# Hybrid decoder layer: the meta tokens' probabilities of four heads turned by one transpose, and the reciprocal sums turned in pairs of heads

## The chip, the cores and the metric

The kernel runs on one core of one Trainium2 chip. The metric is the device time of one execution in microseconds (us); a version's time is the median of several runs.

## The reference

One decoder layer in float32 over 1024 tokens, with 16 learned meta tokens put ahead of them. One input projection feeds two mixers side by side: a chunkwise retention (4 heads) and a sparse attention (8 query heads of 64, one shared key and value head). For every query the sparse attention picks 256 keys by an indexer's score and softmaxes over these alone. An output projection and a squared-ReLU MLP follow. What the change touches is the last line of the attention:

```
logits = jnp.where(valid[:, :, None, :], logits + bias, NEG)
p = jax.nn.softmax(logits, axis=-1)
return jnp.einsum('bchk,bckd->bchd', p, v_sel)
```

The kernel does not gather: it masks the keys that were not selected and works over all earlier keys. So for a block of 128 queries the probabilities P are a 128 x n matrix per head, and the output is P times the values, divided by the row sums of P. The first 16 columns of P belong to the meta tokens, which every query sees.

## The kernel before, in words

**Precision.** Matmuls take a reduced float32 format (fp32r), so most operands are split into a high and a low half, and products are summed from two or three matmuls. The values are kept as `vv`, where a row is (high half | low half), 128 columns. A product with `vv` as the stationary operand gives a 128-row result whose upper and lower 64 rows are added at the end.

**Units of the attention.** The 1024 queries are 8 blocks (i = 0 to 7) and the 8 heads are 2 groups of four (g), which makes 16 units. Each unit has two parts. `attend_p(i, g)` makes P of four heads: matmuls (L580, L581), a masked sum with a running minimum on DVE (L582), an exponential with row sums on ACT (L589), and at the end the reciprocals of the four row sums (L592). `attend_v(i, g)` applies the values. Per tile of keys it transposes the four heads' P on PE (L607), rounds the result to the high half on ACT (L615), takes the rest as the low half on DVE (L616), and multiplies both with `vv` (L617, L619) into one PSUM accumulator `pv`.

**The meta tile.** The first tile of every unit, k = 0, holds the 16 meta tokens (b = 8). Its four transposes have 16 columns each and give a 16 x 512 tile. The high half lies in rows 0 to 15 of a 128 x 512 buffer `pm` and the low half in rows 32 to 47; the rest of `pm` is zero from a memset. `vv[:, 8]` has the meta values in the same two row groups, so that one matmul does both halves. This matmul opens the accumulator (`start=True`); those of all the other tiles come behind it.

**The tail of a unit.** Four transposes (L623) spread the four reciprocals, 128 equal columns each, over a 128 x 512 PSUM tile `rb`. Then for each of two halves: ACT copies one half of `pv` into `ytmp` (L629), DVE adds the other (L630), and DVE multiplies with the reciprocals into the output `y` (L631). `ytmp` is a tile in the pool `small` under a tag with a single buffer.

**Order of the work.** Unit u's `attend_p` is issued together with unit u-1's `attend_v` and, in 10 of the rounds, with one piece of the output projection (`out_piece`, L669 to L671: 24 matmuls of 512 columns). A helper `spread` interleaves their steps. The rounds u = 2, 3, 6 and 8 have no such piece. On top of that the framework orders the instructions of each engine itself, by priority and readiness in its own simulation, and hands out the buffers of a tag; the resulting order on each engine is fixed. PSUM has 8 banks: 3 for `psA` (scores), 5 for `psB` (`pv`, transposes, `rb`, the projection). The two units of block 0 run their `attend_v` side by side in round 2.

**Set-up.** `small_proj` makes `vv` early, for b = 8 from the meta tokens' projection (L283 to L286). `rsqrt(kss, 9)` (L425) norms the keys. The bias load (L433) is one DMA on SP's queue.

Of the kernel before, what the change touches and what calls it, by code (L numbers as in the profile page):

```python
# [9 lines left out]
F32 = mybir.dt.float32  # L10
F32R = mybir.dt.float32r
BF = mybir.dt.bfloat16
I32 = mybir.dt.int32
AF = mybir.ActivationFunctionType
ALU = mybir.AluOpType
# [5 lines left out]
NM = 16  # L21
ML = 32
# [59 lines left out]
def layer(ctx, tc, x, meta, norm1_w, w_in, ret_w, q_w, k_w, rel, w_out, norm2_w, w1, w2,  # L82
          ident_d, pack_d, hot_d, out, gam):
    nc = tc.nc
    const = ctx.enter_context(tc.tile_pool(name="const", bufs=1))
    wp = ctx.enter_context(tc.tile_pool(name="wp", bufs=1))
    small = ctx.enter_context(tc.tile_pool(name="small", bufs=2))
# [6 lines left out]
    big = stage.enter_context(tc.tile_pool(name="p1", bufs=1))  # L94
# [11 lines left out]
    def page(shape, dt, name):  # L106
        return pg.tile(shape, dt, tag="pg", name=name, bufs=8)
# [7 lines left out]
    def row(name, shape=(128, D)):  # L115
        return big.tile(list(shape), F32, tag="row", name=name, bufs=3)
# [10 lines left out]
    ident = const.tile([128, 128], F32, name="ident")  # L127
# [10 lines left out]

    def rsqrt(ms, k, f=1.0, P=128):
        y = small.tile([128, k], F32, name="rs_y", tag=f"rsy{k}", bufs=1 if k == 9 else 4)  # L140
        nc.gpsimd.tensor_tensor(y[:P], ms, epst[f][:P, :k] if isinstance(f, float) else f, op=ALU.add)
        nc.gpsimd.tensor_tensor(y[:P], y[:P], nhalf[:P, :k], op=ALU.pow)
        return y

    def norm_T(src, P, dst, u=None):
        ss = small.tile([128, 1], F32, name="ss")
        if u is None:
            u = row("u")
        nc.scalar.activation(u[:P, :D], src, AF.Square, scale=D ** -0.5, accum_out=ss[:P])
        r = rsqrt(ss[:P], 1, 1.0, P)  # L150
        nc.vector.scalar_tensor_tensor(u[:P, :D], src, r[:P], nrow[:P], op0=ALU.mult, op1=ALU.mult)
# [109 lines left out]
    NS = 200  # L261
    kn = big.tile([128, 9, 64], F32, name="kn")
    vv = kp_.tile([128, 9, 128], F32R, name="vv")
    nc.vector.memset(vv[:, 8].bitcast(F32), 0.0)
    absw = px.tile([128, NB, 8], F32, name="absw")
    sgnw = px.tile([128, NB, 8], F32, name="sgnw")
    w8 = px.tile([128, NB, 8], F32, name="w8")
    kss = const.tile([128, 9], F32, name="kss")
    nc.vector.memset(kss, 1.0)

    def small_proj(b, hs, ls):
        P = NM if b == 8 else 128
        if b == 8:
            s = proj_meta(hs, ls, 0, NS, "oh", 3)
        else:
            ps = psA()
            proj(ps, b, hs, ls, 0, NS)
            s = big.tile([128, NS], F32, name="smp", tag="fg", bufs=2)
            nc.scalar.activation(s, ps[:, :NS], AF.Copy)
        jk64 = jk[:, :64]  # L280
        nc.scalar.activation(jk64[:P], s[:P, 72:136], AF.Square, scale=0.125, accum_out=kss[:P, b:b + 1])
        nc.vector.tensor_copy(kn[:P, b], s[:P, 72:136])
        nc.scalar.activation(vv[:P, b, 0:64], s[:P, 136:200], AF.Copy)  # L283
        nc.vector.tensor_tensor(vv[:P, b, 64:128], s[:P, 136:200], vv[:P, b, 0:64].bitcast(F32), op=ALU.subtract)
        if b == 8:
            nc.scalar.activation(vv[ML:ML + NM, b], vv[:NM, b].bitcast(F32), AF.Copy)  # L286
        if b < 8:
            nc.vector.tensor_scalar(w8[:, b], s[:, 64:72], 8.0 ** -0.5, None, op0=ALU.mult)
            nc.vector.scalar_tensor_tensor(absw[:, b], w8[:, b], -1.0, w8[:, b], op0=ALU.mult, op1=ALU.max)
            nc.scalar.activation(sgnw[:, b], w8[:, b], AF.Sign)  # L290
        return s
# [127 lines left out]
    ap_ = att.enter_context(tc.tile_pool(name="att", bufs=1, side="right"))  # L419
    knh = ap_.tile([128, KW], F32R, name="knh")  # L420
    knl = ap_.tile([128, KW], F32R, name="knl")
    bias = ap_.tile([128, 8, WIN], F32, name="bias")
    pm = ap_.tile([128, 512], F32R, name="pm")
    nc.gpsimd.memset(pm.bitcast(F32), 0.0)
    kr = rsqrt(kss, 9)  # L425
    for b in range(9):
        P = NM if b == 8 else 128
        nc.vector.scalar_tensor_tensor(kn[:P, b], kn[:P, b], kr[:P, b:b + 1], kgain[:P], op0=ALU.mult, op1=ALU.mult)
# [2 lines left out]
        key_T([(kn[:, b], 128) for b in range(4 * t, 4 * t + 4)], NM + 512 * t, knh, knl, -1.0)  # L431
    gap = gd[:]
    nc.sync.dma_start(bias, bass.AP(tensor=gap.tensor, offset=gap.offset + 127, ap=[[8 * L - 1, 128], [L, 8], [1, WIN]]))  # L433


    yrd = dr.tile([128, NB, 512], F32, name="yrd")
# [79 lines left out]
    for b in range(NB):  # L516
# [9 lines left out]
        r = rsqrt(ssq, 8, 64.0)  # L526
# [9 lines left out]
    for i in range(NB):  # L536
        n = ncol[i]
# [3 lines left out]
    at = {}  # L541
    kc = [0]
# [19 lines left out]
    def attend_p(i, g):  # L562
        n = ncol[i]
        win = wins[i]
        mb = at["m"][:, g]
        u = 2 * i + g
        nc.gpsimd.tensor_tensor(mb[:, :, :win], bias[:, 4 * g:4 * g + 4, WIN - win:],
                                sc[i][:, None, n - win:].to_broadcast([128, 4, win]), op=ALU.add)
        P = []
        sums = small.tile([128, 4], F32, name="sums")  # L570
        rs = small.tile([128, 4], F32, name="rs")
        for hh in range(4):
            per = 4 if i < 3 else 2
            if hh % per == 0:
                pp2 = (page if u < 4 or u % 4 >= 2 and i >= 3 else page_b)([128, per, n if i < 7 else 1056], F32, "P")
            p = pp2[:, hh % per]
            mn = small.tile([128, len(segs[i])], F32, name="mn", tag=f"mn{len(segs[i])}")
            for k, (c0, w, last) in enumerate(segs[i]):
                ps = psA()
                nc.tensor.matmul(ps[:, :w], qst[i][:, 4 * g + hh, :], knh[:, c0:c0 + w], start=True, stop=False)  # L580
                nc.tensor.matmul(ps[:, :w], qst[i][:, 4 * g + hh, :], knl[:, c0:c0 + w], start=False, stop=True)  # L581
                nc.vector.tensor_tensor_reduce(  # L582
                    out=p[:, c0:c0 + w], in0=ps[:, :w], in1=mb[:, hh, :win] if last else sc[i][:, c0:c0 + w],
                    scale=1.0, scalar=3e38, op0=ALU.add, op1=ALU.min, accum_out=mn[:, k:k + 1])
            m1 = mn
            if len(segs[i]) > 1:
                m1 = small.tile([128, 1], F32, name="m1")
                nc.vector.tensor_reduce(m1, mn, axis=mybir.AxisListType.X, op=ALU.min)
            nc.scalar.activation(p[:, :n], p[:, :n], AF.Exp, scale=-1.0, bias=m1, accum_out=sums[:, hh:hh + 1])  # L589
            P.append(p)  # L590
            yield
        nc.vector.reciprocal(rs, sums)  # L592
        res[i, g] = P, rs

    res = {}

    def attend_v(i, g):
        P, rs = res.pop((i, g))
        if g == 0:
            ydsa[i] = p2["p"].tile([128, 4, 128], F32, tag="yd", name="yd", bufs=4) if i else ap_.tile([128, 4, 128], F32, name="yd0")  # L600
        y = ydsa[i]
        pv = psB()
        tiles = [(8, 0, NM)] + [(b, NM + 128 * b, 128) for b in range(i + 1)]
        for k, (b, k0, kp) in enumerate(tiles):
            tp = psB()
            for hh in range(4):
                nc.tensor.transpose(tp[:kp, 128 * hh:128 * hh + 128], P[hh][:, k0:k0 + kp], ident)  # L607
            if "h" not in at:
                at["h"] = [page([128, 4, 512], F32R, "ph")]
            kc[0] += 1  # L610
            e = kc[0] % 2
            ph, pl = at["h"][e // 2][:, e % 2], at["h"][e // 2][:, 2 + e % 2]
            if b == 8:
                ph, pl = pm, pm[ML:]
            nc.scalar.activation(ph[:kp], tp[:kp], AF.Copy)  # L615
            nc.vector.tensor_tensor(pl[:kp], tp[:kp], ph[:kp].bitcast(F32), op=ALU.subtract)  # L616
            nc.tensor.matmul(pv, vv[:, b, :], ph, start=k == 0, stop=False)  # L617
            if b < 8:
                nc.tensor.matmul(pv, vv[:, b, :], pl, start=False, stop=k == len(tiles) - 1)  # L619
            yield  # L620
        rb = psB()
        for hh in range(4):
            nc.tensor.transpose(rb[:, 128 * hh:128 * hh + 128], rs[:, hh:hh + 1].to_broadcast([128, 128]), ident)  # L623
        r4 = rb.rearrange("p (c e n) -> p c e n", c=2, e=2)
        p4 = pv.rearrange("p (c e n) -> p c e n", c=2, e=2)
        tmp = small.tile([128, 2, 128], F32, name="ytmp", tag="ytmp", bufs=1)
        for e in range(2):
            a, z = (slice(0, 64), slice(64, 128)) if e == 0 else (slice(64, 128), slice(0, 64))
            nc.scalar.activation(tmp[a], p4[z, :, e], AF.Copy)  # L629
            nc.vector.tensor_tensor(tmp[a], p4[a, :, e], tmp[a], op=ALU.add)  # L630
            nc.vector.tensor_tensor(y[a, 2 * g:2 * g + 2], r4[a, :, e], tmp[a], op=ALU.mult)  # L631

    nrow = const.tile([128, D], F32, name="nrow2", tag="nrow")
    nc.sync.dma_start(nrow, bcast(norm2_w, D))
# [194 lines left out]
    for u in range(2, 2 * NB):  # L829
        i, g = u // 2, u % 2  # L830
# [73 lines left out]
    big = ctx.enter_context(tc.tile_pool(name="p3", bufs=1, side="right"))  # L904
# [242 lines left out]
    for n in range(len(units)):  # L1147
# [4 lines left out]
        if 3 <= n < 7:  # L1152
            s = slice(128 * (n - 3), 128 * (n - 3) + 128)
# [50 lines left out]
```

## Time and profile before

| what | value |
|---|---|
| median of 3 runs | 1323.49 us (1321.75 to 1327.82) |
| the profiled execution's own time | 1322.03 us |
| its span in the trace | 1320.3 us |
| PE, PEld, DVE, ACT, POOL busy | 95%, 79%, 79%, 58%, 19% |
| mean granted clock of PE | 0.986 |

The profile shows one execution. PE is the matmul engine, PEld its weight loads, DVE, ACT and POOL are the vector, scalar and general engines, and SP issues the DMAs. A busy share says how long an engine had an instruction running. Every engine takes its instructions in a fixed order, so an instruction that waits holds up those behind it on the same engine. Durations of matmuls contain their latency, and neighbouring ones overlap; what one costs in a stream is the distance from start to start. "L607" is line 607 of the kernel.

### The profile page before, as it was taken

Reading aid. Unit: us, or ns where it says so; the run is one execution under the profiler, and the core shown is the slowest. Engines: PE = TensorE matmul, PEld = TensorE weight load, DVE = VectorE, ACT = ScalarE, POOL = GpSimd, SP = SyncE. Lnnn points to the kernel's source line nnn. Section 1 sums busy time; section 2 is a strip of 40 time slices with the busy share of each in tenths; the row PEclk is TensorE's granted clock in tenths of the full one; section 3 lists DMA queues with packets and bytes.
Section 4 is the critical chain, followed back from the end, with each engine's and each line's share of the span. In section 5 each row is a group of like instructions: output and inputs, shape, how many; then the busy total and the mean of one; then the engine's idle time right before and its main releaser. Section 6 shows DMA issues by size and latency. Waiting matters only on the chain. (4 is left out here: it accounts for less than half of the span.)

```text
span 1320.3 us, 18430 instructions
## 1 busy us (share of the span) xinstructions
PE 1254.5 (95%) x6144; PEld 1036.8 (79%) x6144; DVE 1038.5 (79%) x2277; ACT 767.3 (58%) x1588; POOL 253.5 (19%) x298
## 2 busy tenths in 40 slices
PE   5999989999999899999987999999999999999998
PEld 4888867877877677787775888888887888888887
DVE  5589999995458888776769877777778988887875
ACT  6567466887875668565746555554546444444442
POOL 4003472425335333210333000000000200000000
PEclk9999989999999999999997999999999999999999
DMA  8103031202112111212543343443538834444222
GB/s 275 59 17 90 22 91 63 72 9 72 35 55 74 66 62 56 65 47 74 179 149 112 141 159 131 150 159 131 177 144 303 342 141 168 151 144 177 94 96 96
DMA packets 94046, 153.46 MB, mean 116 GB/s; under 512 B 7752, under 2 KB 47856, under 8 KB 90240
## 3 DMA queue, kind: packets, MB, share of 16 engines
q1 hardware_dynamic: 93952, 152.29, 33.4%
q8 instruction: 48, 0.79, 0.2%
q14 instruction: 46, 0.38, 0.1%
HBM read 110.32 MB, written 43.46 MB: 116 GB/s over the span
## 5 line engine op out<-in xcount | busy, mean ns | idle before, releaser
L955 ACT ACTIVATE wh<-ga 128x512 fp32r<-128x512 f32 x144 | 87.3, 628 | 157.6 <-PE psB L1103 142.9
L246 PE MATMUL psA<-wh,uh 128*128 128x512 f32 x376 | 151.7, 404 | 3.5 <-DVE fg L481 2.2
L247 PE MATMUL psA<-wh,ul 128*128 128x512 f32 x376 | 149.2, 397 | 0.0
L248 PE MATMUL psA<-wl,uh 128*128 128x512 f32 x376 | 148.7, 396 | 0.0
L956 DVE TENSOR_TENSOR wl<-ga,wh 128x512 fp32r<-128x512 f32 x144 | 96.5, 686 | 47.4 <-ACT wh L955 46.8
L955 ACT ACTIVATE wh<-sum 128x512 fp32r<-128x512 f32 x128 | 78.7, 625 | 80.1 <-DVE sum L952 75.6
L723 ACT ACTIVATE jk_top<-sc,tcand 128x784 bf16<-128x784 f32 (+2 forms) x93 | 98.3, 1057 | 23.9 <-DVE tcand L793 19.8
L1103 PE MATMUL psB<-wh,wl 128*128 128x512 f32 x280 | 109.0, 389 | 0.9 <-DVE wl L956 0.9
L1104 PE MATMUL psB<-wl,wh 128*128 128x512 f32 x280 | 108.9, 389 | 0.0
L1102 PE MATMUL psB<-wh 128*128 128x512 f32 x280 | 106.8, 389 | 0.0
L956 DVE TENSOR_TENSOR wl<-sum,wh 128x512 fp32r<-128x512 f32 x128 | 87.5, 684 | 6.2 <-ACT wh L955 6.2
L246 PEld LDWEIGHTS psA<-wh,uh 128*128 128x128 f32 x376 | 71.3, 190 | 17.6 <-DVE fg L481 1.9
L1022 POOL COPY ga<-wl 128x1 f32<-128x1 f32 x8 | 6.6, 826 | 404.8 <-DVE wl L956 361.4
L248 PEld LDWEIGHTS psA<-wl,uh 128*128 128x128 f32 x376 | 71.2, 190 | 13.9
L247 PEld LDWEIGHTS psA<-wh,ul 128*128 128x128 f32 x376 | 71.4, 190 | 12.2
L718 DVE TENSOR_SCALAR_CACHE_REDUCE jk_cnt<-sc,tcand 128x400 bf16<-128x400 f32 (+2 forms) x93 | 70.3, 756 | 1.0
L194 POOL TENSOR_TENSOR wl<-wr,wh 128x512 fp32r<-128x512 f32 x48 | 67.0, 1418 | 18.4 <-ACT wh L189 12.3
L358 ACT ACTIVATE rl<-psB,absw 128x320 f32<-128x320 f32 (+5 forms) x104 | 53.0, 555 | 28.5 <-DVE sc L362 15.9
L1103 PE MATMUL psA<-wh,wl 128*128 128x512 f32 x168 | 65.4, 389 | 0.0
L1104 PE MATMUL psA<-wl,wh 128*128 128x512 f32 x168 | 65.4, 389 | 0.0
L1102 PE MATMUL psA<-wh 128*128 128x512 f32 x168 | 64.9, 389 | 0.0
L952 DVE TENSOR_TENSOR sum<-wr,wr 128x512 f32<-128x512 f32 x48 | 31.7, 686 | 41.5 <-DMA wr<-in_w_ff_dram 36.0
(392 smaller groups left out, 3642.7 us busy)
## 6 DMA issues: line engine op xcount, KB each, us to landing
ga<-hid SPq DMA_DIRECT2D x28, 1024.0 KB, 5.0
wr<-in_w_ff_dram SPq DMA_DIRECT2D x34, 512.0 KB, 5.0
hid<-hs SPq DMA_DIRECT2D x48, 256.0 KB, 2.0
wr<-in_w_in_dram SPq DMA_DIRECT2D x32, 256.0 KB, 3.1
gb<-in_w_ff_dram SPq DMA_DIRECT2D x8, 1024.0 KB, 5.0
ga<-in_w_ff_dram SPq DMA_DIRECT2D x8, 1024.0 KB, 5.9
wr<-in_w_out_dram SPq DMA_DIRECT2D x12, 512.0 KB, 4.1
xt<-in_x_dram SPq DMA_DIRECT2D x8, 512.0 KB, 4.4
```

Of the source, the lines that this page charges most:

```text
L194: e.tensor_tensor(shl, raw, shp.bitcast(F32), op=ALU.subtract)
L246: nc.tensor.matmul(ps[:P, :n], uh, wh, start=d == 0, stop=False)
L247: nc.tensor.matmul(ps[:P, :n], ul, wh, start=False, stop=False)
L248: nc.tensor.matmul(ps[:P, :n], uh, wl, start=False, stop=d == 7)
L358: nc.scalar.activation(r[:, :w], ps[:, :w], AF.Relu, scale=absw[:, i, h:h + 1])
L718: nc.vector.tensor_scalar(jk_[:, :ncol[i]], sc[i], cand[:, j:j + 1], 0.0, op0=ALU.is_ge, op1=ALU.add, accum_out=cnt[:, j:j + 1])
L723: nc.scalar.activation(jk_top[:, :ncol[i]], sc[i], AF.Sign, scale=-1.0, bias=cand[:, j:j + 1], accum_out=cnt[:, j:j + 1])
L955: nc.scalar.activation(view(hi), s, AF.Copy)
L956: nc.vector.tensor_tensor(view(lo), s, view(hi).bitcast(F32), op=SUB)
L1102: nc.tensor.matmul(ps[tb], ah[:, t], bh, start=j == 0 and m not in CONT, stop=False, skip_group_check=True)
L1103: nc.tensor.matmul(ps[tb], al[:, t], bh, start=False, stop=False, skip_group_check=True)
L1104: nc.tensor.matmul(ps[tb], ah[:, t], bl, start=False, stop=j == NO - 1, skip_group_check=True)
```

## The change

In `attend_v`, the meta tile of a unit is now made like this. Two ACT copies write the 16 meta columns of the four heads, each twice, next to each other into a 128 x 128 tile `few` (column order: head, copy, token). One transpose turns it, so that a PSUM tile has 32 rows per head: 16 rows for the first copy and 16 for the second. ACT rounds it into `few[:, 1]`. Four DVE instructions, one per head, write the 32 rows of that head into its own 128 columns of `pm`: `odd` is 1 in the rows of the second copy and 0 in those of the first, so the first copy gives minus the high half and the second the low half. The rest of `pm` stays zero: it is a matrix of four diagonal blocks. `vv[:, 8]` now holds the meta values eight times, with a minus sign in every other group of 16 rows, filled by eight small DMAs from a tile `vm2`. One matmul over `pm` still does all of it.

In the tail, ACT spreads the four reciprocals into `rx` (128 x 4 x 64), two transposes turn it, and one DVE multiplication over 128 x 256 replaces two over 64 x 256. `few` and `rx` are tiles under the tag of `ytmp`, which still has one buffer. The meta tile no longer takes a turn of the two `ph` buffers.

```diff
-    nc.vector.memset(vv[:, 8].bitcast(F32), 0.0)
+    vm2 = big.tile([128, 2, 128], F32R, tag="eq", name="vm2", bufs=1)
...
-            nc.scalar.activation(vv[ML:ML + NM, b], vv[:NM, b].bitcast(F32), AF.Copy)
+            nc.scalar.activation(vm2[:NM, 0], v.bitcast(F32), AF.Copy, scale=-1.0)
...
+    odd = kss[:, 9:10]
+    nc.vector.tensor_reduce(odd, ident.rearrange("p (a r k) -> p a r k", r=2, k=NM)[:, :, 1], axis=mybir.AxisListType.XY,
+                            op=ALU.add)
...
+    for a in range(8):
+        nc.sync.dma_start(vv[NM * a:NM * a + NM, 8].bitcast(F32), vm2[:NM, a % 2].bitcast(F32))
...
             tp = psB()
-            for hh in range(4):
-                nc.tensor.transpose(tp[:kp, 128 * hh:128 * hh + 128], P[hh][:, k0:k0 + kp], ident)
...
             if b == 8:
-                ph, pl = pm, pm[ML:]
-            nc.scalar.activation(ph[:kp], tp[:kp], AF.Copy)
-            nc.vector.tensor_tensor(pl[:kp], tp[:kp], ph[:kp].bitcast(F32), op=ALU.subtract)
-            nc.tensor.matmul(pv, vv[:, b, :], ph, start=k == 0, stop=False)
...
+                few = small.tile([128, 2, 128], F32R, name="few", tag="ytmp", bufs=1)
+                for e in range(2):
+                    nc.scalar.activation(few[:, 0, 64 * e:64 * e + 64].bitcast(F32).rearrange("p (h r k) -> p h r k", h=2, r=2),
+                                         pairs[e].to_broadcast([128, 2, 2, NM]), AF.Copy)
+                nc.tensor.transpose(tp[:, :128], few[:, 0].bitcast(F32), ident)
+                nc.scalar.activation(few[:, 1], tp[:, :128], AF.Copy)
+                for hh in range(4):
+                    z = slice(32 * hh, 32 * hh + 32)
+                    nc.vector.scalar_tensor_tensor(pm[z, hh], tp[z, :128], odd[z], few[z, 1].bitcast(F32),
+                                                   op0=ALU.mult, op1=ALU.subtract)
+                nc.tensor.matmul(pv, vv[:, 8], pm.rearrange("p h n -> p (h n)"), start=True, stop=False)
...
         rb = psB()
-        for hh in range(4):
-            nc.tensor.transpose(rb[:, 128 * hh:128 * hh + 128], rs[:, hh:hh + 1].to_broadcast([128, 128]), ident)
-        r4 = rb.rearrange("p (c e n) -> p c e n", c=2, e=2)
+        rx = small.tile([128, 4, 64], F32, name="rx", tag="ytmp", bufs=1)
+        nc.scalar.activation(rx, rs[:, :, None].to_broadcast([128, 4, 64]), AF.Copy)
+        for c in range(2):
+            nc.tensor.transpose(rb[:, 128 * c:128 * c + 128], rx[:, 2 * c:2 * c + 2].rearrange("p e n -> p (e n)"), ident)
...
-            nc.vector.tensor_tensor(y[a, 2 * g:2 * g + 2], r4[a, :, e], tmp[a], op=ALU.mult)
+        nc.vector.tensor_tensor(y[:, 2 * g:2 * g + 2], rb[:, :256].rearrange("p (c n) -> p c n", c=2), tmp, op=ALU.mult)
```

## Rows read from the trace of the kernel before

**Rows 1.** Page, part 2: tenths of 40 equal slices; attention is slices 14 to 20.
```profile
PE   5999989999999899999987999999999999999998
...
PEclk9999989999999999999997999999999999999999
```

**Rows 2.** Windows: stretch, length, busy us (count) of PE, PEld, DVE, ACT, POOL; clock; DMA.
```profile
429.00:470.00 41.00, 34.88 (x213) 28.08 (x212) 34.42 (x141) 26.92 (x71) 13.59 (x8) 1.00 0.24 77
470.00:630.00 160.00, 152.85 (x894) 126.12 (x893) 123.77 (x384) 101.79 (x200) 37.10 (x24) 1.00 0.18 58
```

**Rows 3.** Waits of 429 to 660 us: waiter <- releaser: total us, times, longest.
```profile
PEld psB L617 <- DVE pm L616: 7.8, 15, 1.2
...
PE psB L617 <- DVE pm L616: 3.9, 12, 0.9
...
PEld psB L617 <- ACT ph L615: 1.5, 2, 1.0
```

**Rows 4.** Groups by shape, 429 to 660 us: busy us, mean ns, idle before.
```profile
L631 DVE TENSOR_TENSOR yd<-psB,ytmp 64x256 f32<-64x256 f32 x32 | 13.4, 420 | 0.7
...
L629 ACT ACTIVATE ytmp<-psB 64x256 f32<-64x256 f32 x32 | 12.1, 378 | 4.9 <-DVE ytmp L630 2.9 <-PE psB L619 1.4
...
L616 DVE TENSOR_TENSOR pm<-psB,pm 16x512 fp32r<-16x512 f32 x16 | 10.9, 680 | 0.7 <-ACT pm L615 0.2
...
L615 ACT ACTIVATE pm<-psB 16x512 fp32r<-16x512 f32 x16 | 9.3, 582 | 4.1 <-PE psB L607 3.9
```

**Rows 5.** Timeline, one stream of PE: start us, length us, merged instructions (xcount).
```profile
435.95 1.03 PE L607 MATMUL psB<-ident,P 128*128 128x128 f32 x8
...
436.82 0.60 PE L623 MATMUL psB<-ident,rs 128*128 128x128 f32 x4
```

**Rows 6.** Groups by shape ahead of 430 us: shapes nearest to the added instructions.
```profile
L491 ACT ACTIVATE qkT<-psB 128x256 f32<-128x256 f32 x32 | 12.3, 383 | 1.4 <-PE psB L489 1.3
...
L503 DVE SCALAR_TENSOR_TENSOR S<-S,psB 128x128 f32<-128x128 f32 x28 | 7.7, 276 | 0.0
...
L283 ACT ACTIVATE vv<-smp 128x64 fp32r<-128x64 f32 x8 | 2.0, 246 | 0.0
...
L464 ACT ACTIVATE S<-psB 128x128 f32<-128x128 f32 x4 | 1.0, 262 | 0.0
```

**Rows 7.** Timeline, 500 to 511 us: tail of unit (3, 0), head of (3, 1).
```profile
500.29 0.60 PE L623 MATMUL psB<-ident,rs 128*128 128x128 f32 x4
...
501.60 0.59 ACT L615 ACTIVATE pm<-psB 16x512 fp32r<-16x512 f32 x1 [1.24 <-PE psB L607]
...
503.24 0.51 PE L617 MATMUL psB<-pm,vv 128*128 128x512 f32 x1
...
510.62 0.43 DVE L631 TENSOR_TENSOR yd<-psB,ytmp 64x256 f32<-64x256 f32 x1
```

**Rows 8.** Timeline: next unit's head and unit's last L631, at three more boundaries of units.
```profile
440.76 0.59 ACT L615 ACTIVATE pm<-psB 16x512 fp32r<-16x512 f32 x1
...
449.28 0.43 DVE L631 TENSOR_TENSOR yd<-psB,ytmp 64x256 f32<-64x256 f32 x1
...
477.06 0.59 ACT L615 ACTIVATE pm<-psB 16x512 fp32r<-16x512 f32 x1 [1.60 <-PE psB L607]
...
483.19 0.43 DVE L631 TENSOR_TENSOR yd<-psB,ytmp 64x256 f32<-64x256 f32 x1
...
627.68 0.59 ACT L615 ACTIVATE pm<-psB 16x512 fp32r<-16x512 f32 x1
...
631.54 0.43 DVE L631 TENSOR_TENSOR yd<-psB,ytmp 64x256 f32<-64x256 f32 x1
```

**Rows 9.** Timeline of SP's queue, 29 to 45 us, after the meta values are made.
```profile
30.88 0.37 SPq L214 DMA_DIRECT2D wr<-in_w_in_dram  x1
37.95 0.34 SPq L181 DMA_DIRECT2D xt<-in_x_dram  x1
```

**Rows 10.** Timeline of DVE at the start: its first idle time.
```profile
9.33 0.37 DVE L327 TENSOR_TENSOR wsl<-wrs,wsh 128x200 fp32r<-128x200 f32 x1 [7.77 <-ACT wsh L326]
```

More of the change, by code (lines that the diff above doesn't have):

```diff
@@ L267, in layer @@
     w8 = px.tile([128, NB, 8], F32, name="w8")
-    kss = const.tile([128, 9], F32, name="kss")
+    kss = const.tile([128, 10], F32, name="kss")
     nc.vector.memset(kss, 1.0)
@@ L282, in small_proj @@
         nc.vector.tensor_copy(kn[:P, b], s[:P, 72:136])
-        nc.scalar.activation(vv[:P, b, 0:64], s[:P, 136:200], AF.Copy)
-        nc.vector.tensor_tensor(vv[:P, b, 64:128], s[:P, 136:200], vv[:P, b, 0:64].bitcast(F32), op=ALU.subtract)
+        v = vm2[:NM, 1] if b == 8 else vv[:, b]
+        nc.scalar.activation(v[:P, 0:64], s[:P, 136:200], AF.Copy)
+        nc.vector.tensor_tensor(v[:P, 64:128], s[:P, 136:200], v[:P, 0:64].bitcast(F32), op=ALU.subtract)
         if b == 8:
-            nc.scalar.activation(vv[ML:ML + NM, b], vv[:NM, b].bitcast(F32), AF.Copy)
+            nc.scalar.activation(vm2[:NM, 0], v.bitcast(F32), AF.Copy, scale=-1.0)
         if b < 8:
@@ L422, in layer @@
     bias = ap_.tile([128, 8, WIN], F32, name="bias")
-    pm = ap_.tile([128, 512], F32R, name="pm")
+    pm = ap_.tile([128, 4, 128], F32R, name="pm")
     nc.gpsimd.memset(pm.bitcast(F32), 0.0)
-    kr = rsqrt(kss, 9)
+    odd = kss[:, 9:10]
+    nc.vector.tensor_reduce(odd, ident.rearrange("p (a r k) -> p a r k", r=2, k=NM)[:, :, 1], axis=mybir.AxisListType.XY,
+                            op=ALU.add)
+    kr = rsqrt(kss[:, :9], 9)
     for b in range(9):
@@ L568, in attend_p @@
                                 sc[i][:, None, n - win:].to_broadcast([128, 4, win]), op=ALU.add)
-        P = []
+        P, pairs = [], []
         sums = small.tile([128, 4], F32, name="sums")
@@ L576, in attend_p @@
             p = pp2[:, hh % per]
+            if hh % 2 == 0:
+                pairs.append(pp2[:, hh % per:hh % per + 2, None, :NM])
             mn = small.tile([128, len(segs[i])], F32, name="mn", tag=f"mn{len(segs[i])}")
@@ L592, in attend_p @@
         nc.vector.reciprocal(rs, sums)
-        res[i, g] = P, rs
+        res[i, g] = P, pairs, rs
     res = {}
     def attend_v(i, g):
-        P, rs = res.pop((i, g))
+        P, pairs, rs = res.pop((i, g))
         if g == 0:
@@ L605, in attend_v @@
             tp = psB()
-            for hh in range(4):
-                nc.tensor.transpose(tp[:kp, 128 * hh:128 * hh + 128], P[hh][:, k0:k0 + kp], ident)
[L608 to L612, printed above, removed]
-            if b == 8:
-                ph, pl = pm, pm[ML:]
-            nc.scalar.activation(ph[:kp], tp[:kp], AF.Copy)
-            nc.vector.tensor_tensor(pl[:kp], tp[:kp], ph[:kp].bitcast(F32), op=ALU.subtract)
-            nc.tensor.matmul(pv, vv[:, b, :], ph, start=k == 0, stop=False)
-            if b < 8:
+            if b == 8:
+                few = small.tile([128, 2, 128], F32R, name="few", tag="ytmp", bufs=1)
[9 more added lines that the diff above has]
+                nc.tensor.matmul(pv, vv[:, 8], pm.rearrange("p h n -> p (h n)"), start=True, stop=False)
+            else:
+                for hh in range(4):
+                    nc.tensor.transpose(tp[:, 128 * hh:128 * hh + 128], P[hh][:, k0:k0 + kp], ident)
+                if "h" not in at:
+                    at["h"] = [page([128, 4, 512], F32R, "ph")]
+                kc[0] += 1
+                ph, pl = at["h"][0][:, kc[0] % 2], at["h"][0][:, 2 + kc[0] % 2]
+                nc.scalar.activation(ph, tp, AF.Copy)
+                nc.vector.tensor_tensor(pl, tp, ph.bitcast(F32), op=ALU.subtract)
+                nc.tensor.matmul(pv, vv[:, b, :], ph, start=False, stop=False)
                 nc.tensor.matmul(pv, vv[:, b, :], pl, start=False, stop=k == len(tiles) - 1)
```

## The prediction, made before the changed kernel ran

> **What bounds the kernel now.** I read the page's slices first: PE is busy nine tenths or more nearly everywhere and its granted clock stays near full [rows 1]. So PE's work is the first suspect, but a share over the whole span says nothing of the stage that is changed. That stage is the attention, from 429 to about 660 us. The windows show it in two parts: from 429 to 470 us PE is busy 34.88 of 41 us and DVE 34.42, so neither is the bound alone; from 470 to 630 us PE is busy 152.85 of 160 us (95.5%), DVE 123.77 and ACT 101.79, at clock 1.00 [rows 2]. In the second part PE is the bound, with short holes. The waits tell which holes belong to the changed lines: PE waited 3.9 us in 12 pieces, and its weight loads 7.8 us in 15 pieces, for the low half of `pm` [rows 3]. These two overlap, so the meta tile's matmul costs about 4 us of standing PE in 16 units.
>
> **The change, part by part.**
>
> *Transposes.* Eight transposes of 128 columns show 1.03 us together and four show 0.60 us; the first of the eight starts 0.87 us before the four, which is 8 times 0.109 us [rows 5]. So one transpose costs 0.109 us of the stream. A unit loses three at the meta tile and two in the tail: 5 times 0.109 = 0.545 us, times 16 units 8.7 us. Eleven units have their meta matmul after 470 us (the heads from 477.06 to 627.68 us [rows 8]); I count 95.5% of their share, 11 times 0.545 times 0.955 = 5.7 us. The five earlier ones lie where DVE is as busy as PE; I count half, 1.4 us. Gain: **7.1 us**, bounds 4 (half of all) and 8.7.
>
> By the Trainium skill, "TensorE: Matmul & The Clock Gate", section "Back-to-back issue gap", a matmul of 128 columns takes 134 cycles, about 56 ns, in a stream. By that the gain would be half of mine, an estimate of 4.5 us over 16 units. The row shows 109 ns for these transposes, and the measurement decides.
>
> *DVE.* Removed per unit: one subtraction of 680 ns and one of the two multiplications of 420 ns [rows 4]. Added: four operations of 128 elements from PSUM at 276 ns, the row of the same operation at that width [rows 6], 1.10 us. They have 32 rows instead of 128; the rows at hand go with the width, not the height (16 rows by 512 take 680 ns, 64 by 256 take 420, 128 by 128 take 276). The multiplication that stays covers the same 256 elements. Sum 1.10 - 0.68 - 0.42 = 0. Bounds per unit: four at a quarter of the old 680 ns is -0.42, four at the 420 of the wider one is +0.58; I take the row in between.
>
> *ACT.* Removed per unit: 582 ns [rows 4]. Added: two copies of 64 elements at 246, one of 128 at 262 and one of 256 at 383 ns [rows 6], 1.14 us. So ACT gets 0.555 us per unit more, 8.9 us in all. ACT is busy 64% of the second part [rows 2], and weight loads waited for it 1.5 us [rows 3], so most of it falls into idle time; without that cover it would be the whole 8.9. Between 0 and 8.9 I take **1.0 us**, by the nearest row, that wait of 1.5.
>
> *The chain at the head of a unit.* Before: four transposes 0.60, ACT 0.58, DVE 0.68, then the matmul: 1.86 us without gaps; from ACT's start to the matmul the trace has 1.64 us [rows 7], where the durations give 1.26. After: two copies 0.49, a transpose 0.27, ACT 0.26, four DVE operations 1.10: 2.12 us, and one more change of engine. That is about 0.3 us longer. PE already stands for `pm` in most units, and behind this matmul all the other products of the unit's accumulator are queued. But the order on the engines is planned anew, so other matmuls can go first. Between 0 and 16 times 0.5 us I take 0.1 per unit, **1.6 us**.
>
> *The one buffer.* `few`, `rx` and `ytmp` share one buffer. Ahead of a unit's end `rx` must be read by its two transposes before `ytmp` may be written, and the next unit's `few` needs the buffer too. Behind `few` on ACT stand the exponentials of the next `attend_p`, behind its transpose PE's stream. Today the reciprocals' transposes run at 500.29, and the next head's ACT starts at 501.60, well ahead of the old unit's last multiplication at 510.62 [rows 7]. P of the next unit is finished by then, so `few` can take the buffer right behind `rx`, and `ytmp` comes after it; as far as I know the framework gives a free buffer to what is ready. I count **0** for that, the last rival counts the other case.
>
> *Once per kernel.* Eight DMA issues at some 0.4 us each, 3 us on SP. After the meta values are made SP's queue is empty from 31.25 to 37.95 us [rows 9], and it holds them; if they come later they delay stores that nobody waits for soon. The small reduction on DVE and the dropped memset lie in DVE's first idle time of 7.77 us [rows 10]. 0; without that cover below 1 us. POOL keeps its one memset.
>
> *Sum:* -7.1 + 1.0 + 1.6 = -4.5 us. Against the profiled execution's own 1322.0 us that is 1317.5, and against the median of the runs, 1.5 us higher, 1319. I give 1318.
>
> **The rivals.** A measurement here tells about 0.5% from no change: 6.6 us, so below 1316.9 or above 1330.1.
>
> 1. *The full relief.* The new plan puts the meta matmul where it doesn't wait, and the freed PE time is worth all of it: -8.7 and up to -3.9 [rows 3]: 1309.5 to 1315, most likely 1313. For it: PE's 95.5%. Against: the longer chain, and the first part, where DVE is as full.
> 2. *The transposes are not what PE is short of.* If their place is half worth (they overlap weight loads, and holes open where they were) the gain is 4.4 us and the 2.6 us of costs eat most of it: 1322 to 1320. The skill's price for 128 columns, above, would come out the same way. Against: the spacing of 0.109 us stands in the trace.
> 3. *The shared buffer ties units together (slower).* If the next `few` gets the buffer only after the old unit's last multiplication, its head starts later than today by the distance between the two: 8.5 and 6.1 and 9.0 us at three boundaries, 3.9 at the last [rows 7, 8]; over the 14 boundaries from round 3 on it is 2.8 to 9.0. Ten of these rounds have a projection piece, whose 24 matmuls can fill PE meanwhile. The rounds 3, 6 and 8 have none: these are the boundaries with 8.5, 6.1 and 9.0 us, 23.6 together. If half of it is filled by scores and transposes, 11.8 stays, against the 4.5 gained: +7, about 1329.5; if nothing is filled, 1341. It decides from a loss of 0.4 us per unit. For it: one buffer, long tails. Against: P is ready early, and the simulation sees the conflict when it plans.
>
> **How the numbers follow.** Forecast (1316 to 1320.5) 0.40; full relief 0.27; half worth 0.11; shared buffer 0.22. Faster by over 0.5%: nearly all of the relief and a quarter of the forecast, 0.37. Slower by over 0.5%: above 1330.1 lies some 0.14 of the shared buffer's 0.22. Within: 0.49. The range goes from 1310 (the relief's end leaves out some 0.05) to 1330 (0.14 left out).
>
> **What would show it.** In the profile after: 80 fewer matmuls of L607 and L623 kinds; PE's busy time in the attention some 8 us less, and the stage (429 to 660 us) 4 to 7 us shorter while the rest keeps its length; DVE's busy time equal and ACT's up by 9 us; waits of the meta matmul for DVE of 4 to 6 us. Wrong it would be if those waits, or waits of ACT's `few` for the last multiplication, hold more than 10 us (rival 3), if the stage shortens by over 8 us with fewer holes in PE (rival 1), or if PE's idle time grows by what was removed (rival 2).

## The result and the profile after

The changed kernel takes **1399.88 us** (median of 4 runs, 1398.47 to 1402.6), the kernel before 1323.71 us beside it (4 runs). The ratio is 1.0596, with a 95% interval from 1.0577 to 1.0616: 76 us slower. The forecast was 1318, its range ended at 1330.

First the page's parts 1 and 2 of the kernel after (the slices are 35 us long here), and behind them part 1 of the kernel before.

```profile
PE 1286.8 (92%) x6064; PEld 1057.6 (76%) x6064; DVE 1047.8 (75%) x2309; ACT 778.8 (56%) x1636; POOL 251.6 (18%) x298
...
PE   6999989999997777987878799999999999999998
...
PEclk9999989999998777898899899999999999999999
```

```profile
PE 1254.5 (95%) x6144; PEld 1036.8 (79%) x6144; DVE 1038.5 (79%) x2277; ACT 767.3 (58%) x1588; POOL 253.5 (19%) x298
```

The attention is slices 13 to 21 here. Seven of these nine show a PE of 7 or 8, and seven a clock of 7 or 8, where [rows 1] have 9 nearly throughout. The kernel has 80 matmuls fewer (6064 for 6144), as the diff says, and PE was still busy 32 us longer than before (1286.8 for 1254.5). Fewer instructions that take longer: a first sign of the clock.

The windows run from 429 us to the end of the span. They are cut at the end of the attention, which is the end of the last multiplication into `y`, and once more some 80 us behind it: first after, then before (length, then busy us and count of PE, PEld, DVE, ACT, POOL, the clock, DMA).

```profile
429.00:735.33 306.33, 241.77 (x1153) 191.56 (x1152) 186.99 (x584) 161.31 (x356) 60.39 (x44) 0.84 0.16 55
735.33:815.00 79.67, 66.71 (x286) 53.63 (x285) 64.21 (x90) 45.32 (x80) 24.61 (x22) 0.91 0.40 136
815.00:1398.80 583.80, 578.58 (x2550) 477.87 (x2548) 461.31 (x739) 275.19 (x490) 9.27 (x18) 1.00 0.45 163
```

```profile
429.00:656.32 227.32, 211.51 (x1238) 172.76 (x1237) 179.18 (x557) 151.07 (x312) 60.86 (x44) 1.00 0.22 73
656.32:736.00 79.68, 66.84 (x285) 53.51 (x284) 64.58 (x90) 44.97 (x80) 24.71 (x22) 0.89 0.41 137
736.00:1320.30 584.30, 578.59 (x2551) 478.18 (x2549) 461.07 (x739) 275.14 (x490) 9.26 (x18) 1.00 0.45 163
```

The stages behind the attention keep their length to half a microsecond. The attention went from 227.3 to 306.3 us, 79.0 longer, and the two rows split this: PE stood still for 306.33 - 241.77 = 64.6 us instead of 15.8, which is 48.7 us more, and it was busy 30.3 us longer at a mean clock of 0.84 instead of 1.00. As an estimate, 241.77 x 0.84 is 203 us at full clock, and the work of before less the 80 removed transposes is 211.5 - 80 x 0.109 = 202.8 us: by this estimate the clock accounts for the 30 us.

Where PE stands, the timeline shows at the boundary of units (2, 0) and (2, 1). In the kernel before this is the second pair of [rows 8]: there the new head's ACT started 6.1 us ahead of the old unit's last multiplication.

```profile
502.89 0.35 PE L589 MATMUL psA<-knl,qs 128*128 128x416 f32 x1
...
504.54 0.42 DVE L649 TENSOR_TENSOR yd<-psB,ytmp 128x256 f32<-128x256 f32 x1
504.99 0.40 ACT L617 ACTIVATE few<-P 128x64 f32<-128x64 f32 x2 [0.95 <-DVE yd L649]
...
505.45 0.39 PE L619 MATMUL psB<-ident,few 128*128 128x128 f32 x1 [2.21 <-ACT few L617]
505.87 0.28 ACT L620 ACTIVATE few<-psB 128x128 fp32r<-128x128 f32 x1 [0.47 <-PE psB L619]
506.18 1.44 DVE L623 SCALAR_TENSOR_TENSOR pm<-psB,kss,few 32x128 fp32r<-32x128 f32 x4 [1.22 <-ACT few L620]
...
507.67 0.80 PE L625 MATMUL psB<-pm,vv 128*128 128x512 f32 x1 [1.84 <-DVE pm L623]
```

`few` starts when the old unit's last multiplication ends (504.96), not when its P is ready (456.17, the end of its last exponential). Then the chain runs alone, and PE does one transpose between 503.24 and 507.67. The same order, last multiplication first and `few` behind it, stands at all 14 boundaries from round 3 on. At a later boundary the round has a piece of the projection (L687 to L689), and it does not help:

```profile
655.48 0.48 PE L688 MATMUL psB<-wh,ys 128*128 128x512 f32 x1
655.79 0.40 PE L689 MATMUL psB<-wl,ys 128*128 128x512 f32 x1
656.02 0.40 PE L635 MATMUL psB<-ph,vv 128*128 128x512 f32 x1
...
659.85 0.49 PE L636 MATMUL psB<-ph,vv 128*128 128x512 f32 x1
662.12 0.42 DVE L649 TENSOR_TENSOR yd<-psB,ytmp 128x256 f32<-128x256 f32 x1
662.58 0.40 ACT L617 ACTIVATE few<-P 128x64 f32<-128x64 f32 x2 [0.95 <-DVE yd L649]
...
665.44 0.77 PE L625 MATMUL psB<-pm,vv 128*128 128x512 f32 x1 [1.93 <-DVE pm L623]
...
666.00 0.63 PE L687 MATMUL psB<-wh,ys 128*128 128x512 f32 x1
666.43 0.63 PE L688 MATMUL psB<-wh,ys 128*128 128x512 f32 x1
666.85 0.63 PE L689 MATMUL psB<-wl,ys 128*128 128x512 f32 x1
```

PE runs out of work at 660.34 and gets the projection's next matmuls at 666.00. By their operands (`wh`, `wl`, `ys`) they need nothing of the head; they stand behind its transpose and its matmul in PE's fixed order. And they show the clock: from start to start they take 0.43 us, where the same shape took 0.23 us (655.79 to 656.02) ahead of the wait. 512 columns in 0.43 us is the lower of the clock's two levels, 1.2 GHz, instead of 2.4.

The waits of the attention (429 to 740 us) that answer to [rows 3]:

```profile
PE psB L625 <- DVE pm L623: 26.4, 16, 2.5
ACT rx L640 <- DVE pm L623: 21.0, 15, 2.1
PEld psB L619 <- ACT few L617: 18.0, 9, 3.0
PE psB L619 <- ACT few L617: 15.8, 9, 2.7
...
ACT few L617 <- DVE yd L649: 4.3, 6, 1.0
```

The tie itself is the small wait at the end: ACT waits for `yd` only 4.3 us, in 6 pieces, because other instructions of ACT, the copies of the old unit's tail among them, run until just before. PE pays, 15.8 us at the transpose and 26.4 us at the matmul.

And the groups by shape, beside [rows 4] and the prices of [rows 6]:

```profile
L623 DVE SCALAR_TENSOR_TENSOR pm<-psB,kss,few 32x128 fp32r<-32x128 f32 x64 | 22.2, 347 | 13.9 <-ACT few L620 13.1
...
L649 DVE TENSOR_TENSOR yd<-psB,ytmp 128x256 f32<-128x256 f32 x16 | 6.7, 421 | 0.2
L640 ACT ACTIVATE rx<-rs 128x256 f32<-128x256 f32 x16 | 6.6, 415 | 21.0 <-DVE pm L623 21.0
...
L620 ACT ACTIVATE few<-psB 128x128 fp32r<-128x128 f32 x16 | 4.3, 269 | 5.2 <-PE psB L619 5.1
```

### The profile page after: what moved, and what is told of

It reads as the page before. It is cut to its first block, busy times and chain, and to the rows that moved or that the text cites. A ratio compares the mean times of both kernels' runs of the same rounds, so it can differ in the third digit from the quotient of the medians.

```text
span 1398.8 us, 18387 instructions
## 1 busy us (share of the span) xinstructions
PE 1286.8 (92%) x6064; PEld 1057.6 (76%) x6064; DVE 1047.8 (75%) x2309; ACT 778.8 (56%) x1636; POOL 251.6 (18%) x298
## 5 line engine op out<-in xcount | busy, mean ns | idle before, releaser
L634 DVE TENSOR_TENSOR ph<-psB,ph 128x512 fp32r<-128x512 f32 x72 | 49.2, 689 | 65.3 <-ACT ph L633 41.2
L633 ACT ACTIVATE ph<-psB 128x512 fp32r<-128x512 f32 x72 | 42.6, 598 | 64.7 <-PE psB L628 31.6
```

## The experiments

The theories at the start: **A**, the one buffer is handed over in program order and ties each unit's head to the tail before it; **B**, the head's own chain is too long wherever the buffer lies; **C**, a good part of the loss is the granted clock that falls while PE stands. Every kernel ran beside the kernel before on the same chip (medians 1321.9 to 1323.2 us). "r" is the ratio to it with the 95% interval. Where a kernel ran only once, the text says so, and there is no interval.

**few_own.** `few` in places of its own; `rx` and `ytmp` still share the buffer.

```diff
...
-                few = small.tile([128, 2, 128], F32R, name="few", tag="ytmp", bufs=1)
+                few0, few1 = at["few"], um.rearrange("p a b -> p (a b)")[:, 0:128]
...
```

> The changed kernel with one difference: `few` no longer shares ytmp's buffer (its first half lies in the unused end of the page of `mb`, its second half in the dead tile `um`); `rx` and `ytmp` still share. Theory A (the one buffer goes from unit to unit in the order of the program, so a unit's head waits for the last multiplication of the unit before): the tie is gone, 1310 to 1330 us, clock back above 0.98. Theory B (the head's own path, ACT, PE, ACT, four DVE operations, is too long for the stage whatever the buffer): 1380 to 1400 us, as before the difference.

1337.04 us, r 1.0108 (1.0091 to 1.0125): 63 of the 76 us are gone, so the tie through `few` is the main cause (A). 14.5 us stay, more than A had room for and far from what B named; the run's mean clock, 0.976, stayed under A's 0.98 too. The matmul over `pm` still waits:

```profile
PE psB L627 <- DVE pm L625: 18.3, 15, 2.4
```

**head_only_shared.** The new head with the shared buffer, the old tail.

```diff
-        rx = small.tile([128, 4, 64], F32, name="rx", tag="ytmp", bufs=1)
...
+        for hh in range(4):
+            nc.tensor.transpose(rb[:, 128 * hh:128 * hh + 128], rs[:, hh:hh + 1].to_broadcast([128, 128]), ident)
```

> The changed kernel with the old tail: four transposes of the reciprocals and two multiplications, no `rx`; `few` and `ytmp` share the one buffer. Theory A: the tie between units stays, 1380 to 1410 us. A second form of A, in which it is `rx` that holds the buffer (ACT stood 21 us in front of it), gives 1320 to 1350 us. Theory B: 1380 to 1400 us.

1414.26 us in a single run, 4 us above A's range. Without `rx` the loss is all there, and larger: `few` and `ytmp` alone make the tie.

**before_tied.** The kernel before with nothing new but the tie: a factor 1.0, written by ACT into a tile of `ytmp`'s buffer, multiplies into the subtraction that makes `pm`'s low half.

```diff
-            nc.vector.tensor_tensor(pl[:kp], tp[:kp], ph[:kp].bitcast(F32), op=ALU.subtract)
+            if b == 8:
+                one = small.tile([128, 2, 128], F32, name="one", tag="ytmp", bufs=1)
+                nc.scalar.activation(one[:NM, 0, 0:1], ident[:NM, 0:1], AF.Copy, scale=0.0, bias=1.0)
+                nc.vector.scalar_tensor_tensor(pl[:kp], tp[:kp], one[:NM, 0, 0:1], ph[:kp].bitcast(F32),
+                                               op0=ALU.mult, op1=ALU.subtract)
...
```

> The kernel before, with nothing of the change but a tie: at the meta tile ACT writes a single 1.0 into a tile under ytmp's tag, and the DVE subtraction of the meta tile takes it as its factor. The four transposes, the rounding and the tail are the old ones. Theory A: the tie alone makes it slow, 1360 to 1400 us. Theory B: nothing in the head's path got longer but one small ACT instruction, 1322 to 1330 us.

1383.55 us in a single run: a tile of one column in the shared buffer costs the old kernel 61 us. The timeline at the same boundary, (2, 0) to (2, 1):

```profile
500.48 0.43 DVE L637 TENSOR_TENSOR yd<-psB,ytmp 64x256 f32<-64x256 f32 x1
500.94 0.20 ACT L618 ACTIVATE one<-ident 16x1 f32<-16x1 f32 x1 [0.96 <-DVE yd L637]
501.18 0.74 DVE L619 SCALAR_TENSOR_TENSOR pm<-psB,one,pm 16x512 fp32r<-16x512 f32 x1 [0.27 <-ACT one L618]
...
501.97 0.79 PE L623 MATMUL psB<-pm,vv 128*128 128x512 f32 x1 [2.65 <-DVE pm L619]
```

`one` needs nothing but a constant, and it still waits for `yd`. Nothing of the change's own work is in this kernel, so the tie is shown by itself.

**after_filled.** The changed kernel with 12 unread matmuls of 384 columns behind the transpose of `few`, to keep PE busy while it waits.

```diff
+                for _ in range(12):
+                    nc.tensor.matmul(tp[:, 128:512], vv[:, 0], knh[:, 0:384], start=True, stop=True)
```

> The changed kernel plus 12 matmuls of 384 columns per unit, right behind the transpose of `few`, into columns of the same PSUM tile that nobody reads; they add some 12 times 0.16 = 1.9 us of PE work per unit where PE stands and waits for `pm`. Theory C (a good part of the loss is the granted clock, which fell to 0.83 in the stage because PE stands): the clock of the stage rises above 0.95, PE's busy time falls although work was added, 1345 to 1385 us. If the clock is only a companion: 1395 to 1420 us.

1425.35 us in a single run: a miss for C, though the mean clock of 470 to 630 us rose to 0.93 (0.85 in the changed kernel). But the filler lay in the PSUM tile that ACT reads next, and ACT waited for it (36.0 us for `few` on PE, 5.1 in the changed kernel). It lengthened the chain that it was to lie beside, so this run does not decide about C.

**after_pvfill and few_own_pvfill.** A better filler: eight unread matmuls of 512 columns into the accumulator, ahead of the matmul that opens it anew. In the changed kernel and in few_own.

```diff
+                for _ in range(8):
+                    nc.tensor.matmul(pv, vv[:, 0], knh[:, 0:512], start=True, stop=True)
                 nc.tensor.matmul(pv, vv[:, 8], pm.rearrange("p h n -> p (h n)"), start=True, stop=False)
```

> The changed kernel with eight unread matmuls of 512 columns into the accumulator of the unit, ahead of the matmul over pm that opens it anew: about 1.7 us of matmul work per unit, 27 us in all, which depend on nothing in the head's chain. Theory C (a good part of the 76 us is the granted clock, which falls because PE stands at each head): the clock of 470 to 630 us comes above 0.95 and the time to 1350 to 1390 us although PE has 27 us more to do. Against C (the waits alone are the loss): the fill lies in the waits or beside them, 1395 to 1427 us, the clock may rise or not.

> The same eight unread matmuls in few_own (1337.0 us, granted clock 0.976). Theory C: clock 0.985 or more and 1325 to 1338 us, that is no dearer in spite of 27 us more matmul work. Against C: 1340 to 1365 us.

A single run each: 1385.15 us (the changed kernel: 1399.88) and 1324.43 us (few_own: 1337.04). Both got faster with 128 matmuls more, 27 us of work by the expectation (29 at the 0.23 us of the rows above). The first is in C's range, and its mean clock of 470 to 630 us was 0.93 instead of 0.85, under the 0.95 that C asked for. The second is just below C's range, with 1.00 instead of 0.98. few_own's was timed again:

> The kernel of few_own_pvfill again, now timed in rounds. If the single look was right, 1322 to 1328 us, 9 to 15 us under few_own's 1337.0; if it was chance, 1333 to 1342.

1328.0 us, r 1.0034 (1.0020 to 1.0049): 9 us under few_own, with intervals well apart, so the single run was 3.6 us low but right in kind. The matmul over `pm` waits 0.4 us for DVE instead of 18.3:

```profile
PE psB L629 <- DVE pm L625: 0.4, 1, 0.4
```

What this does not separate: with the filler the framework orders the attention's PE work anew, so the clock and the new order come together.

**before_pvfill.** The control: the same filler in the kernel before, first in a single run, then timed in eight.

> Control for the two runs with unread matmuls: the kernel before with the same eight matmuls of 512 columns ahead of the meta tile's matmul, 27 us of work. There PE stands little and the granted clock is 1.00 in the attention. Theory C (the unread work pays only where PE stands and the clock falls): 1333 to 1350 us here, that is dearer than the kernel before, while few_own got 12.6 us faster by it. If unread work were free in any case, 1320 to 1326 us.

> The control again, timed in rounds: 27 us of unread matmul work in the kernel before. If PE's work sets this stage's time, as the forecast's term for the transposes had it (0.955 of each us removed), 1340 us or more; if PE has room here, 1325 to 1331 us, that is under a quarter of the added work shows.

1327.93 us, and timed 1326.62, r 1.0029 (1.0017 to 1.0041): 27 us of work cost 3.8 us by the ratio (4.4 by the medians). The first expectation was missed on both sides, the second hit on the side against the forecast. The attention itself ends 6.8 us later in the trace (663.1 for 656.3 us), and the stage behind it gives a part back. So PE had room for three quarters of the work or more, in a stage whose PE was "busy" 95.5% [rows 2]; that is also more than the 15.8 us in which it stood still. The windows of before_pvfill_timed:

```profile
429.00:470.00 41.00, 40.95 (x254) 34.82 (x253) 32.30 (x128) 25.47 (x67) 14.78 (x9) 1.00 0.22 70
470.00:630.00 160.00, 158.39 (x939) 135.51 (x937) 125.07 (x389) 101.69 (x197) 36.31 (x24) 1.00 0.17 57
```

**tail_only.** The kernel before with the new tail alone (`rx`, two transposes, one multiplication), no `few`.

> The kernel before with the new tail alone: reciprocals spread by ACT into rx, two transposes instead of four, one multiplication of 128x256; rx takes the buffer of ytmp, there is no few. If the remaining 14.5 us of few_own come from the head's own longer chain (copy, transpose, rounding, four DVE operations, matmul; theory B), the tail alone costs nothing: 1316 to 1324 us, granted clock 0.985 or more. If they come from rx and ytmp taking turns in one buffer (theory A, second part), this kernel shows them: 1332 to 1340 us, with waits of ACT's rx for the multiplication of the unit before over 10 us.

1324.74 us, r 1.0018 (1.0005 to 1.0031). This is just above the first range. 32 transposes fewer, 3.5 us by their spacing, and the time is 2.4 us longer; `rx` waits only 1.1 us for the old unit's last multiplication. The new tail is nearly harmless, and it gains nothing.

**head_only_own.** The new head with `few` in its own places, the old tail.

> The new head with few in places of its own, and the old tail (four transposes of the reciprocals, two multiplications). Theory B (the head's own chain): 1330 to 1342 us, and the matmul over pm waits over 12 us for DVE in the attention. Theory A, second part (rx and ytmp): 1318 to 1327 us. If both have a share, each of this run and tail_only lies 5 to 9 us above the kernel before.

1342.33 us, r 1.0169 (1.0145 to 1.0192), at the upper end of B's range, and the matmul over `pm` waits 17.2 us for DVE, as B asked. So the 14.5 us of few_own are the head's own chain (B), not `rx` and `ytmp`; with the old tail they are even 20.

**after_meta_second, after_meta_last, few_own_meta_second.** The order of a unit's tiles: the first key tile goes ahead of the meta tile (in the second kernel all key tiles do), and the meta tile adds to the accumulator instead of opening it.

```diff
-        tiles = [(8, 0, NM)] + [(b, NM + 128 * b, 128) for b in range(i + 1)]
+        tiles = [(b, NM + 128 * b, 128) for b in range(i + 1)]
+        tiles.insert(1, (8, 0, NM))
...
```

> The changed kernel with the first key tile of a unit ahead of its meta tile, which now adds to the accumulator instead of opening it; buffers as in the changed kernel. Theory A (few waits for the old unit's last multiplication, and the unit's other products stand behind the matmul over pm): the first key tile, some 1.9 us of PE's work with its own rounding, now runs in that time, so a part of the loss goes: 1345 to 1385 us. Rival (the tie stops the unit wherever few stands): 1390 to 1410 us.

> The changed kernel with the meta tile as the last tile of its unit. Theory A: few then has the whole unit to get its buffer, so the tie is off the path and only the tail's own chain stays: 1316 to 1340 us, clock over 0.975. Rival (the chain of few only moves to the unit's end, where rx and ytmp must wait for it in the one buffer): 1350 to 1400 us, with waits of ACT's rx or ytmp for DVE's pm over 20 us in the attention.

> few_own with the first key tile ahead of the meta tile. Theory B (the remaining 14.5 us of few_own are the head's own chain, five steps on three engines with nothing else of the unit ready): the chain lies beside the first key tile, waits of the matmul over pm for DVE under 8 us, 1314 to 1327 us. If the chain isn't what costs, 1332 to 1342 us as few_own.

In this order: 1336.87 us, r 1.0097 (1.0060 to 1.0134); 1340.45 us, r 1.0125 (1.0096 to 1.0155); 1321.19 us, r 0.9980 (0.9964 to 0.9996). With the buffers untouched, the order of two tiles gives back 63 of the 76 us, more than was expected. The tie costs because the tied instructions stood first in the unit. Meta last is no better and just misses theory A's range: `rx` still waits 19.8 us for `pm`, nearly the 21.0 of the changed kernel. And few_own, its chain off the path, comes to the time of the kernel before. Its waits of 429 to 760 us:

```profile
PEld psB L628 <- DVE pm L626: 7.7, 8, 1.6
PE psB L628 <- DVE pm L626: 6.3, 7, 1.4
```

**before_meta_second and head_own_meta_second.** The new order in the kernel before, with nothing else; and in the new head with its own places and the old tail.

> Control: the kernel before with the first key tile ahead of the meta tile and nothing else changed. If the gain of few_own_meta_second over the kernel before (2 us) is the order's, this has it too or more: 1316 to 1321 us. If it is the removed transposes', this one stays at 1322 to 1326 us or gets slower.

> The new head with few in places of its own, the first key tile ahead of it, and the old tail. The tail alone cost 2.4 us in tail_only, and the head off the path removes 48 transposes of 0.109 us, 5.2 us: 1314 to 1320 us if these add up; 1321 to 1326 us if PE's work is worth little in this stage and the rest evens out.

1317.33 us, r 0.9959 (0.9943 to 0.9974), and 1322.56 us, r 0.9999 (0.9985 to 1.0013). The order alone gains 5 us, and the version with the new head has lost them again: the two intervals, from one set of runs on one chip, lie apart. So the new head costs 5.2 us even where nothing ties it, with 48 transposes fewer. DVE carries more there (first head_own_meta_second, then before_meta_second):

```profile
470.00:630.00 160.00, 151.47 (x866) 126.50 (x865) 132.78 (x424) 104.39 (x224) 36.08 (x24) 0.98 0.19 63
470.00:630.00 160.00, 153.34 (x890) 128.53 (x889) 123.73 (x378) 103.29 (x200) 34.22 (x23) 0.97 0.20 63
```

PE is busy 1.9 us less and DVE 9.1 us more. That DVE's time is where the 5.2 us go is not shown. before_meta_second beats both the kernel before, by 0.4%, and the changed one.

## Why the prediction was wrong

**The step that failed is "The one buffer".** It said that "`few` can take the buffer right behind `rx`, and `ytmp` comes after it; as far as I know the framework gives a free buffer to what is ready. I count 0". The buffer went round in the order of the program instead: `rx`, `ytmp`, then the next `few`, at all 14 boundaries. before_tied prices that at 61 us with one column of data, few_own at 63 us by taking it away. In the kernel before, the buffer has one user, `ytmp`, so no row there shows which it would be, and the step took the value 0 from a belief about the framework, not from a row. The bound from the other side stood in the third rival, where it had its place and a chance of 0.22.

**The third rival had the mechanism and a tenth of the price**, +7 (worst case 1341). Three parts of its sum were wrong. First, it counted three boundaries, on the ground that the 24 projection matmuls of the other rounds (eleven, with the last one) "can fill PE meanwhile". They cannot: PE's order is fixed, and they stand on both sides of the waiting transpose (the rows at 655 to 667 us). Over all 14 boundaries of the trace before, the distances that the rival measured add up to 80 us, the size of the loss; that the two agree so well is at least in part luck, since scores and transposes fill some of each and the two points that follow come on top. Secondly, it counted from the old place of the head to the old unit's end, and left out that the chain from `few` to the matmul, 2.7 us at (2, 0) to (2, 1), is then bare too. PE stood still 48.7 us longer over the stage. Thirdly, it had no term for the clock: by the estimate above, 30 us of the 79 are PE at 0.84 instead of 1.00. Of the two signs that the text named for this rival, the waits of the matmul over `pm` came (26.4 us); ACT's `few` itself waits only 4.3 us for the last multiplication, since ACT has other instructions until just before.

By the Trainium skill, "Perfetto Trace Analysis", section "Optimization Strategy", the same gap that repeats on the engine that should be full can mean that there isn't room for the next tile's buffer. The trace agrees: at all 14 boundaries `few` starts only behind the release of the one buffer, and over the attention PE waits 15.8 us for `few` and 26.4 us for `pm`.

**The transposes** were forecast at -7.1 us. The count was right, 80 fewer. The rate was not: tail_only removes 3.5 us of them and gains nothing, and before_pvfill_timed adds 27 us of matmuls at a price of 3.8, 14% of it. Carried over to the 8.7 us of the transposes, that is about 1.2 us (2.2 by the end of the attention in the trace), an estimate, well under the lower bound of 4 and under the second rival's half. The step "I count 95.5% of their share" read a busy share as a bound. The profile counts a matmul's latency as busy (one of 512 columns has a length of 0.40 us, where the next starts 0.23 us later), so a stage of short bursts shows a full PE that still takes more. The Trainium skill says so in "Perfetto Trace Analysis", section "Identifying the Most-Contended Engine": the busy share of matmuls is not a good measure of how near PE is to its roof. Here the trace agrees, by 27 us of work for 3.8.

**The chain at the head** was forecast at 1.6 us. few_own measures 14.5 for head and tail without the tie, less what the removed transposes give. A first key tile ahead of the head takes it away, 5 us of it by the order's own gain, and leaves a cost of 5.2 us beside before_meta_second (head_own_meta_second). "Other matmuls can go first" was the reason for the low value; in the plan as it came, the matmul over `pm` opened the accumulator, and the unit's products were behind it. The bound of 16 times 0.5 us was too low as well.

**DVE** was forecast at 0: four operations at 276 ns. They took 347 each, so a unit's sum is 4 x 0.347 - 0.680 - 0.420 = +0.29 us, inside the bounds (+0.58). That "the rows at hand go with the width, not the height" is not what failed, but the choice of the row: the operation at 276 ns has a constant as its factor, the four new ones take theirs from a tile, one value per row. The trace before has both kinds ahead of 430 us:

```profile
L510 DVE SCALAR_TENSOR_TENSOR oh<-psB,rs_y,fg 128x128 f32<-128x128 f32 x28 | 7.8, 340 | 0.7 <-POOL rs_y L142 0.7
...
L298 DVE SCALAR_TENSOR_TENSOR ikl<-psB,ikh 64x128 fp32r<-64x128 f32 x16 | 4.5, 280 | 0.2
```

L510 has its factor from a tile and 128 rows, and takes 340 ns; L298 has a constant, 64 rows and the fp32r output of the new operations, and takes 280.

**ACT** was right: 2 x 0.245 + 0.269 + 0.415 - 0.582 is 0.59 us per unit for the forecast 0.555. **Once per kernel** was right: the first score matmul starts at 415.0 us for 415.3, and the stages behind the attention kept their length.

## What to carry to other kernels

Before a new tile joins a tag with one buffer, list all the users of that tag in program order and take the worst case, which came true here: each waits until the one before it is read, also across units, and whatever stands behind it in an engine's fixed order waits with it. If the buffer must be shared, put work that doesn't need it first in the unit; here the order of two tiles was worth 63 us. And do not price work removed from PE by PE's busy share: add work and see what it costs, which is one run.

## What the hardware showed that was not expected

- **A wait of PE makes the work behind it slower too.** After 5.7 us of near standstill the projection matmuls of 512 columns came every 0.43 us instead of 0.23. Over the attention the mean granted clock was 0.84 instead of 1.00, by estimate about 30 of the 79 us lost.
- **Added work made a kernel faster:** few_own 1337.0 us, with 27 us of unread matmuls 1328.0. How much of it is the clock and how much the new order of PE's work stays open.
- **A DVE operation with its factor from a tile takes 60 to 70 ns longer than with a constant.** At 128 columns with an operand in PSUM it took 340 ns on 128 rows (L510) and 347 on 32 (L623), with a constant 280 on 64 rows (L298) and 276 on 128 [rows 6]. No run changed the factor alone, but neither the rows nor the output type sorts these four.
